# The odd layer's entry in a written-out order: x's norm first, ctx's residuals behind it, keys and values projected tile by tile with weights kept

## The chip, the cores and the metric

The kernel runs on one core of a Trainium2 chip. The metric is the device time of one execution in microseconds (us): the median of several runs. Beside it there is one profiled execution, in which the start and the length of nearly every instruction were recorded. Five engines work side by side, each through its own instructions in order: TensorE (PE, the matmuls, with the weight loads shown as PEld), VectorE (DVE), ScalarE (ACT), GpSimd (POOL) and SyncE (SP, which here only issues transfers).

## What is computed

Two transformer layers on x (512 tokens) and ctx (256 tokens), width 1024, all in float32. The layer that matters here is the second, odd one, and the end of the first one's FFN in front of it:

```python
def modulate(x, g, shift, scale):
    return rmsnorm(x, g) * (1 + scale) + shift

for l in range(2):
    ...
    a  = modulate(h,  norm1_g[l], sh1,  sc1)          # x, 512 tokens
    ac = modulate(hc, norm1_g[l], csh1, csc1)         # ctx, 256 tokens
    y, yc = even_mixer(...) if l % 2 == 0 else odd_mixer(a, ac, w_qkv, w_out, sink, cos, sin, need_ctx)
    h = h + g1 * y
    h = h + g2 * swiglu(modulate(h, norm2_g[l], sh2, sc2), ffn_w_in[l], ffn_w_out[l])
    if need_ctx:                                      # l == 0 only
        hc = hc + cg1 * yc
        hc = hc + cg2 * swiglu(modulate(hc, ...), ffn_w_in[l], ffn_w_out[l])
return rmsnorm(h, final_g)

def odd_mixer(h, hc, ...):                            # 16 query heads, 4 key/value heads, 64 wide
    q, k, v = split(h @ w_qkv)                        # rope on q and k
    kc, vc = split(hc @ w_qkv[:, 1024:])              # ctx: keys and values only, no rope
    # softmax over: keys within 128 tokens of the query (mask), all ctx keys, one sink logit per head
    ...
```

## The kernel before, in words

**Matmuls.** Every float32 product is made of three matmuls on a high and a low half in a reduced format: `mm3` (lines 106, 107, 108) multiplies high by high, high by low, low by high into one PSUM bank. An operand thus needs a high half (a cast, mostly on ScalarE) and a low half (source less high half, on VectorE or GpSimd). Activations lie transposed, eight tiles of 128 channels by 512 (x) or 256 (ctx) tokens: `hx[m]` and `hc[m]`, shown in the trace as `xT` and `ctxT`.

**Banks.** PSUM has 3 banks of tag `b` (`bank()`, shown as `pb`), 1 of tag `f` (`fill()`, `pf`), and a pool `wp` with either 2 double banks (`wide()`) or 4 single ones (`single()`), both shown as `pw`. Who asks for a bank waits until the last reader of its former content is done.

**Weights.** `unit` (line 71, called by `blocks`) loads 512 columns of a weight through SyncE into a raw buffer (`raw`, 3 of them in the odd layer's ring), casts the high half on ScalarE (line 81) and subtracts on GpSimd (line 84) into one of 4 slots (`w`). A slot comes free when its last matmul is done.

**Order.** A scheduler with a model of the engines orders most instructions within each engine. The first layer's FFN is ordered by hand instead: `run(key, fn, ...)` issues an instruction behind the last one of the same key (engine).

**The seam.** The FFN's output projection is accumulated in groups of two hidden tiles; the result of each is scaled and added to the residual by `residual` (line 774, VectorE). The units of the last hidden tile are given by a string: "e" to "j" stand for early parts of the last output group, one output tile each (`t` units, x and ctx), in which the last but one hidden tile is multiplied. Then `s2_part` does what is left of the eight x tiles and the eight ctx tiles; each is followed by `square` (line 787 on ScalarE, line 791 adds the first four to a running sum). `modulated` makes the norm, first x, then ctx: `rstd_diag` sums over channels with matmuls against ones (lines 156 and 161), forms the reciprocal root on VectorE with some small operations (lines 164, 135 and three times 137 to 139), multiplies the identity by each column of it (line 173), and `spread` (line 183) turns this with one matmul into rows over all partitions; `modulate` makes each of the eight tiles from it: `t` on VectorE (line 199), the high half on ScalarE (line 200), the low half on VectorE (line 201), shown as `ax`.

**The odd layer's entry.** For each of two key tiles `project_k` loads and splits the eight blocks of its weight, projects x and then ctx into one `wide()`, and makes rope (`rope`: shuffle, line 251, and product with cos, line 252, on VectorE; product with sin and sum, lines 253 and 254, on GpSimd) and the stacked halves (`stack_k`: `kh` on ScalarE, lines 276 and 277, `kl` on VectorE, line 279). Then the values of six token blocks are accumulated in three banks and copied out (line 1328). `project_q` (eight times) does the same as `project_k` for a query tile, with one `fill()` and `stack_q` (`qa`, `qb`, lines 261, 262 and 267). The attention follows, group by group, `softmax` (scores, line 1360 and on, mask, line 1365, maximum, line 1371, exponential, line 1374) and `attend`, with the query projections of later groups between.

Of the kernel before, what the change touches and what calls it, by code (L numbers as in the profile page):

```python
# [14 lines left out]
P = 128  # L15
# [11 lines left out]
class Builder:  # L27
# [12 lines left out]
    def load(self, pool, src, shape, name, dtype=F32, eng=None, bufs=1):  # L40
        t = pool.tile(shape, dtype, name=self.uid(name), tag=name, bufs=bufs)
        (eng or self.nc.sync).dma_start(t, src)
        return t

    def bank(self):
# [812 lines left out]
    def ffn(self, l):  # L858
# [14 lines left out]
        todo = [(1, j, k) for j in range(6) for k in range(KT)] if both else []  # L873
        tail, tiles = {}, []

        def run(key, fn, *args, **kw):

            with tc.issue_after(tail[key].ins) if key in tail else ExitStack():
                tail[key] = fn(*args, **kw)  # L879
            return tail[key]  # L880

# [165 lines left out]

        def s2_part(fs, m, W, off, n, chain=False):
            ps = self.bank()[:, :n]
# [176 lines left out]
        for u in units:  # L1226
# [10 lines left out]
            elif u[0] == "t":  # L1237
                m = u[1]
                for off, n in whos:
                    s2_part((NF - 2,), m, Wl[m][:1], off, n, True)  # L1240
            else:
                unit(*u)
            job()
        ahead = sum(u[0] == "t" for u in units)
        while jobs:
            job()
        sq = self.sumsq()
        if both:
            self.A = [self.ax() for _ in range(KT)]
        parts = ((0, TX), (TX, TC)) if both else ((TC, TC), (0, TC))  # L1250
        q0 = (4, 5)[l]
        more, sqs = [], []
        for off, n in parts:
            rest = []
            for m in range(KT):
                if m < ahead:
                    s2_part((NF - 1,), m, Wl[m][1:], off, n)
                else:
                    s2_part((NF - 2, NF - 1), m, Wl[m], off, n)
                if off == parts[0][0]:  # L1260
                    sqs.append(Tp.tile([P, 2 * NH], F32, name=self.uid("sqs"), tag="T", bufs=12))
                eng = nc.vector if both and m in (2, 3) else nc.gpsimd
                self.square(sq, m, off, n, rest, q0, sqs[m][:, off:off + n], eng)
            more.append(rest)
        if both:
            for q, (off, n) in zip(more, parts):
                self.modulated(1, sq, off, n, q)
        else:
            self.dg = Tp.tile([P, TX], F32, name="dg")
            rows = [self.final_rows(sq, q, off, n) for q, (off, n) in zip(more, parts)]  # L1270
            for r, (off, n) in zip(rows, parts):
                self.final(r, off, n)
        self.Rf.release()
        ring.release()
        Tp.release()
        if both:
            self.ada_close()

    def odd(self):
        tc, nc, a = self.tc, self.nc, self.a  # L1280
        self.wp.release()
        self.open_wide()
        self.open_ring(512, 3, 4)
        X, C = [[[t[:, c] for t in A] for A in self.A] for c in (slice(0, TX), slice(TX, TA))]
        self.hcp.release()
        Rk = tc.alloc_tile_pool(name="kv1", bufs=1, side="right", reuse_waits="tile")
        Rt = tc.alloc_tile_pool(name="rope1", bufs=1, side="right", reuse_waits="tile")
        self.ropep = Rk
        tabs = [self.load(Rk, a[n], [P, TX], n) for n in ("cos", "sin")]
        mraw = self.load(Rt, a["mask"], [P, 384], "mraw")  # L1290
        mask = Rk.tile([P, 384], F32R, name="mask")
        nc.vector.tensor_copy(mask, mraw)
        identr = Rk.tile([P, P], F32R, name="identr")
        nc.vector.tensor_copy(identr, self.ident)
        nsink = self.load(Rk, a["sink"].partition_broadcast(P), [P, 16], "sink")
        sink = Rk.tile([P, 16], F32, name="sink2")
        nc.vector.tensor_copy(sink, nsink)
        nc.vector.tensor_scalar(nsink, nsink, -1.0, None, ALU.mult)

        K = []  # L1300

        def project_k(n):
            W = self.blocks(a["k1"][n])
            kf = Rt.tile([P, TA], F32, name=self.uid("kf"), tag="kf", bufs=1)
            ps = self.wide()
            for off, T, A in ((0, TX, X), (TX, TC, C)):
                self.dense(ps[:, off:off + T], W, A)
            self.rope(ps[:, :TX], kf[:, :TX], tabs)
            nc.scalar.copy(kf[:, TX:], ps[:, TX:TA])
            K.extend(self.stack_k(kf, Rk, TA, "k1", 8))  # L1310

        for n in range(2):
            project_k(n)

        V = []
        bk = [self.bank() for _ in range(3)]
        acc = [b[:, h * TC:(h + 1) * TC] for b in bk for h in range(2)]
        for kq in range(2):
            W = self.blocks(a["v1"][kq], step=256)
            for i in range(4):  # L1320
                k = kq * 4 + i
                for tb in range(6):
                    A = [X[k][p][:, tb * P:(tb + 1) * P] if tb < 4 else C[k][p][:, (tb - 4) * P:(tb - 3) * P]
                         for p in range(2)]
                    self.mm3(acc[tb], A, W[i], k == 0 and tb % 2 == 0, k == KT - 1)
        for tb in range(6):
            v = Rk.tile([P, TC], F32, name=f"v1_{tb}")
            (nc.vector.tensor_copy if tb % 2 else nc.scalar.copy)(v, acc[tb])
            V.append(v)
        Rt.release()  # L1330
# [10 lines left out]
        def softmax(g, i, rc):  # L1341
# [9 lines left out]
            for x in range(4):  # L1351
# [10 lines left out]
                for b in range(b0, b1):  # L1362
                    if b != i:
                        m0, c = (b - i + 1) * P, st + (b - b0) * P
                        nc.tensor.matmul(ps[:, c:c + P], identr, mask[:, m0:m0 + P], start=False, stop=True,
                                         skip_group_check=True)
# [86 lines left out]
        Rs.release()  # L1453
        Rk.release()
        self.ffn_open(1)
        self.ffn_mod(1, 0)
# [98 lines left out]
```

## Time and profile before

| | |
|---|---|
| runs, us | 1605.66, 1608.77, 1609.75 (median 1608.77) |
| profiled execution, us | 1603.73, span in the profile 1601.9 |
| TensorE busy | 1524.8 us (95% of the span), weight loads 1354.8 |
| VectorE / ScalarE / GpSimd busy | 1076.4 (67%) / 722.9 (45%) / 846.9 (53%) |
| transfers | 162.00 MB, mean 101 GB/s |

The stretch that the change rewrites lies between about 916 and 1030 us from the start of the span: the last units of the FFN to 935, x's and ctx's residuals, squares and norms to 949, keys and values to 987, query projections and the first attention blocks behind that. In a line of a timeline there stand the start, the length, the engine, the line of the source, the operation, what it writes and reads, its shape and the count, and in brackets how long the engine had been idle before and what ended that. PEclk is the clock granted to TensorE as a share of full speed. A line of the waits gives who waited for whom, the total, how many times and the longest.

### The profile page before, as it was taken

The page shows a single profiled execution, that of the slowest core. Times are in us where ns is not written, and L with a number is a line of the kernel's source. Part 1 is how long each engine was busy: PE and PEld are TensorE (multiplying, and loading weights), DVE is VectorE, ACT ScalarE, POOL GpSimd, SP SyncE. Part 2 cuts the span into 40 slices and gives each one's busy share as a digit, 9 for nine tenths or more (in the row PEclk, how much of TensorE's full clock was granted, in tenths as well). Part 3 has the DMA queues.
Part 4 walks back from the last instruction along what each step waited for, and adds up shares of the span by engine and source line. Part 5 has one row for each costly group of instructions (what it writes and reads, how often), then busy time and mean ns, then how long its engine had stood idle before and what let it go on. Part 6 is the DMA issues. An engine that isn't in the chain of part 4 may idle for free.

```text
span 1601.9 us, 24950 instructions
## 1 busy us (share of the span) xinstructions
PE 1524.8 (95%) x9547; PEld 1354.8 (85%) x9547; DVE 1076.4 (67%) x1949; ACT 722.9 (45%) x1472; POOL 846.9 (53%) x574
## 2 busy tenths in 40 slices
PE   6999988999999999999999989999999899999996
PEld 4776877889988898999999978777869799999996
DVE  3720788765687888777676486665667966666656
ACT  2412676553542323332333244556655644444442
POOL 0463211061265767766776415541304688888883
PEclk9999999999999999999999999999999999999998
DMA  8845100033133334434442022110225133323301
GB/s 325 305 145 184 40 8 1 24 121 119 66 95 109 125 119 139 137 122 149 141 137 85 27 65 66 60 34 9 72 80 204 53 102 101 115 86 113 93 14 53
DMA packets 54295, 162.00 MB, mean 101 GB/s; under 512 B 6176, under 2 KB 10656, under 8 KB 46496
## 3 DMA queue, kind: packets, MB, share of 16 engines
q1 hardware_dynamic: 47120, 135.11, 25.3%
q10 hardware_dynamic: 7056, 25.30, 4.9%
q8 instruction: 75, 1.23, 0.3%
q14 instruction: 44, 0.36, 0.1%
HBM read 158.29 MB, written 2.10 MB: 100 GB/s over the span
## 4 chain that ended last, share of the span: by engine, by line
PE 79%; DVE 13%; ACT 3%; issue 3%; DMA 1%; POOL 0%; SPq 0%; POOLq 0%; DVEq 0%; ACTq 0%
PE pw L106 11%; PE pw L107 11%; PE pw L108 10%; PE pb L107 8%; PE pb L106 8%; PE pb L108 8%; PE pf L106 4%; PE pf L107 4%; PE pf L108 4%; DVE junk L228 3%; PE pb L1408 2%; PE pb L1397 2%; PE pf L359 2%; PE pw L1360 1%; DMA ar<-ada 1%
## 5 line engine op out<-in xcount | busy, mean ns | idle before, releaser
L84 POOL TENSOR_TENSOR w<-raw,w 128x512 fp32r<-128x512 f32 (+1 forms) x84 | 128.0, 1530 | 241.9 <-ACT w L81 219.2
L106 PE MATMUL pw<-ax,w 128*128 128x384 f32 (+2 forms) x732 | 233.9, 323 | 4.4 <-ACT ax L200 1.6
L107 PE MATMUL pw<-ax,w 128*128 128x384 f32 (+2 forms) x732 | 234.7, 321 | 2.0 <-DVE ax L466 1.4
L108 PE MATMUL pw<-ax,w 128*128 128x384 f32 (+2 forms) x732 | 233.7, 320 | 1.4 <-DVE w L944 1.4
L774 DVE SCALAR_TENSOR_TENSOR xT<-pb,mod,xT 128x512 f32<-128x512 f32 (+3 forms) x208 | 145.8, 706 | 118.2 <-PE pb L108 118.0
L879 POOL TENSOR_TENSOR w<-raw,w 128x512 fp32r<-128x512 f32 x114 | 179.6, 1590 | 39.6 <-ACT w L879 39.4
L879 POOL TENSOR_TENSOR w<-t,w 128x512 fp32r<-128x512 f32 x102 | 157.1, 1544 | 60.9 <-ACT w L879 60.9
L106 PE MATMUL pb<-hh,w 128*128 128x512 f32 x480 | 172.5, 359 | 7.8 <-DVE xT L774 5.2
L107 PE MATMUL pb<-hh,w 128*128 128x512 f32 x480 | 172.4, 359 | 3.5 <-POOL hh L123 2.8
L108 PE MATMUL pb<-hh,w 128*128 128x512 f32 x480 | 172.2, 359 | 0.0
L107 PE MATMUL pw<-T,w 128*128 128x384 f32 (+1 forms) x508 | 157.1, 310 | 1.2 <-DVE T L123 1.2
L108 PE MATMUL pw<-T,w 128*128 128x384 f32 (+1 forms) x508 | 157.1, 310 | 0.0
L106 PE MATMUL pw<-T,w 128*128 128x384 f32 (+1 forms) x508 | 156.4, 310 | 0.0
L106 PEld LDWEIGHTS pw<-ax,w 128*128 128x128 f32 x732 | 139.1, 191 | 12.9 <-ACT ax L200 2.4
L107 PEld LDWEIGHTS pw<-ax,w 128*128 128x128 f32 x732 | 139.4, 191 | 10.2 <-DVE ax L466 3.1
L106 PE MATMUL pf<-ax,w 128*128 128x256 f32 (+2 forms) x420 | 139.9, 333 | 8.3 <-DVE qf L252 5.5
L108 PEld LDWEIGHTS pw<-ax,w 128*128 128x128 f32 x732 | 139.4, 191 | 4.1 <-DVE w L944 1.7
L108 PE MATMUL pf<-ax,w 128*128 128x256 f32 (+2 forms) x420 | 138.8, 330 | 0.0
L107 PE MATMUL pf<-ax,w 128*128 128x256 f32 (+2 forms) x420 | 138.8, 330 | 0.0
L228 DVE SCALAR_TENSOR_TENSOR junk<-ar,cb 128x1024 bf16<-128x1024 f32 x64 | 111.1, 1735 | 8.7 <-DMA ar<-ada 8.1
L879 POOL TENSOR_TENSOR w<-rawo,w 128x512 fp32r<-128x512 f32 x60 | 108.9, 1816 | 11.9 <-ACT w L879 11.9
L879 DVE TENSOR_TENSOR hs<-hs,pw 128x384 f32<-128x384 f32 (+1 forms) x114 | 55.2, 484 | 87.3 <-PE pw L108 74.8
(377 smaller groups left out, 3938.0 us busy)
## 6 DMA issues: line engine op xcount, KB each, us to landing
raw<-ffn_in SPq DMA_DIRECT2D x44, 1024.0 KB, 5.0
ar<-ada SPq DMA_DIRECT2D x24, 1024.0 KB, 7.0
ar<-ada ACTq DMA_DIRECT2D x48, 512.0 KB, 3.5
rawo<-ffn_out SPq DMA_DIRECT2D x88, 256.0 KB, 3.0
raw<-odd_out SPq DMA_DIRECT2D x32, 256.0 KB, 2.7
raw<-qk SPq DMA_DIRECT2D x16, 256.0 KB, 7.8
raw<-uv SPq DMA_DIRECT2D x16, 256.0 KB, 2.7
raw<-even_out SPq DMA_DIRECT2D x8, 512.0 KB, 3.5
```

The lines of the kernel that those rows point to most:

```text
L84: eng.tensor_tensor(lo, raw, hi.bitcast(F32), ALU.subtract)
L106: mm(out, s[0], m[0], start=start, stop=False, **kw)
L107: mm(out, s[0], m[1], start=False, stop=False, **kw)
L108: return mm(out, s[1], m[0], start=False, stop=stop, **kw)
L228: return self.nc.vector.scalar_tensor_tensor(junk, t, 1.0, self.cb[who], ALU.mult, ALU.mult, accum_out=self.acc[who][:, col:col + 1])
L359: nc.tensor.matmul(ps[32 * q:32 * q + 32, :w], cst[:, k, :], t[:, w * q:w * q + w], start=k == 0, stop=k == KT - 1, skip_group_check=True)
L774: ins = self.nc.vector.scalar_tensor_tensor(h, ps[:, r], self.modcol(l, j, m, who), h, ALU.mult, ALU.add)
L879: tail[key] = fn(*args, **kw)
L1360: nc.tensor.matmul(ps[:, st:en], Q, K[g][p][:, b0 * P:b1 * P], start=p == 0, stop=p == 1, skip_group_check=True)
L1397: last = nc.tensor.transpose(pt[:, x * P:(x + 1) * P], es[2 * (x % 2) + x // 2][:, kb * P:(kb + 1) * P], self.ident)
L1408: nc.tensor.matmul(po[64 * h:64 * h + 64, :], V[vb][:, 64 * g:64 * g + 64], t[:, h * TC:h * TC + TC], start=kb == 0, stop=kb == nb - 1, sk ...
```

## The change

*FFN's end.* The string becomes "…s7s4efgh": four `t` units instead of six, of x alone, behind the last unit "4". What is left is done in a new `seam`: the eight x tiles with residuals and squares; ctx tiles 0 to 2 into the three banks of tag `b` (without their residuals); x's channel sums and root (`norm_root`, whose small operations have their scratch in the PSUM bank, but for the result); ctx residuals and squares 0 to 2; ctx tiles 3 to 6 into the four `single()` banks and tile 7 into a `bank()`. Everything in it is issued through `run`, thus in the order written, per engine.

*The entry.* Two rings are open at the same time, the old one (3 raw, 4 slots) for the query weights and a new one (4 raw, 8 slots) for keys and values. The eight halves of key and value weights are kept in the eight slots. The first four are loaded and split ahead of x's `norm_spread`, which makes the four products with the identity on ScalarE; the other four are loaded and split along with x's tiles. Tile by tile, x is modulated, followed by a ctx residual (tiles 0 to 4), and multiplied into both key accumulators and (tiles 0 to 3 at once, 4 to 7 later) into the values' accumulators. Behind tile 5 stands ctx's `norm_root`, behind tile 6 its `norm_spread`. Then ctx is modulated, rope follows, keys and values of ctx come last. The mask is kept as two blocks instead of three, made late with the other constants.

*Queries.* Projection 1 goes into a `bank()` instead of the one `fill()`.

```diff
@@ s2_part
-            run("DVE", self.residual, l, 5, m, off, n, ps)
+            if not late:
+                run("DVE", self.residual, l, 5, m, off, n, ps)
...
-                      ("215s6s3s7sef4ghij", "215s6s3s7sef4g")[l]):
+                      ("215s6s3s7s4efgh", "215s6s3s7sef4g")[l]):
...
-                for off, n in whos:
-                    s2_part((NF - 2,), m, Wl[m][:1], off, n, True)
+                s2_part((NF - 2,), m, Wl[m][:1], 0, TX, True)
...
+    def seam(self, s2_part, Wl, ahead):
...
+        for m in range(KT):
+            k = int(m < ahead)
+            s2_part(fs[k:], m, Wl[m][k:], 0, TX, True)
+            square(0, m)
...
+        for m in range(3):
+            c_unit(m, self.bank())
+        self.rx = self.norm_root(sq[:, :TX], self.rest1[0], TX, self.fill())
+        for m in range(3):
+            self.c_residual(m)
+        for m in range(3, 7):
+            c_unit(m, self.single())
+        c_unit(7, self.bank())
...
+    def norm_spread(self, y, T, out):
+        dg = self.tmp()
+        for j in range(T // P):
+            self.run("ACT", self.nc.scalar.mul, dg[:, j * P:(j + 1) * P], self.ident, y[:, j:j + 1])
+        self.run("PE", self.nc.tensor.matmul, out[:, :T], self.ones, dg[:, :T], start=True, stop=True)
+        return out[:, :T]
@@ odd
+        kept = self.ring, self.ring_cfg
+        self.open_ring(512, 4, 8)
...
+        W = [part(*load(v)) for v in src[:4]]
...
+        rx = self.norm_spread(self.rx, TX, self.fill())
         tabs = [self.load(Rk, a[n], [P, TX], n) for n in ("cos", "sin")]
...
+        for k in range(KT):
+            rest = mod(0, k, rx)
+            if k < 5:
+                self.c_residual(k + 3, Rt)
+            rest()
+            if k < 4:
+                W.append(part(*load(src[4 + k])))
+            k_x(k)
+            if k < 4:
+                v_x(k)
+            if k == 5:
+                rc = self.norm_root(self.sq1[:, TX:], self.rest1[1], TC, self.single())
+            if k == 6:
+                rc = self.norm_spread(rc, TC, self.single())
...
+        for k in range(KT):
+            mod(1, k, rc)()
+            if k >= 4:
+                v_x(k)
+        for n in range(2):
+            self.rope(kps[n], kfs[n][:, :TX], tabs)
+        for k in range(KT):
+            k_c(k)
...
+        for k in range(KT):
+            v_c(k)
...
         def project_q(n):
-            ps = self.fill()
+            ps = (self.bank if n == 1 else self.fill)()
```

More of the change, by code (lines that the diff above doesn't have):

```diff
@@ L1246, in ffn @@
             job()
+        if both:
+            self.seam(s2_part, Wl, ahead)
+            self.Rf.release()
+            ring.release()
+            Tp.release()
+            self.ada_close()
+            return
         sq = self.sumsq()
[L1248 to L1251, printed above, removed]
+        parts, q0 = ((TC, TC), (0, TC)), 5
         more, sqs = [], []
@@ L1261, in ffn @@
                     sqs.append(Tp.tile([P, 2 * NH], F32, name=self.uid("sqs"), tag="T", bufs=12))
-                eng = nc.vector if both and m in (2, 3) else nc.gpsimd
-                self.square(sq, m, off, n, rest, q0, sqs[m][:, off:off + n], eng)
+                self.square(sq, m, off, n, rest, q0, sqs[m][:, off:off + n], nc.gpsimd)
             more.append(rest)
[L1265 to L1272, printed above, removed]
+        self.dg = Tp.tile([P, TX], F32, name="dg")
+        rows = [self.final_rows(sq, q, off, n) for q, (off, n) in zip(more, parts)]
+        for r, (off, n) in zip(rows, parts):
+            self.final(r, off, n)
         self.Rf.release()
@@ L1298, in odd @@
[L1298 to L1310, printed above, removed]
@@ L1312, in odd @@
-        for n in range(2):
-            project_k(n)
-        V = []
[L1316 to L1325, printed above, removed]
+        with tc.issue_after(self.tail["DVE"].ins):
+            nc.vector.tensor_copy(mask, mraw.rearrange("p (a c) -> p a c", a=3)[:, 0::2, :])
+            nc.vector.tensor_copy(identr, self.ident)
+            nc.vector.tensor_copy(sink, nsink)
+            nc.vector.tensor_scalar(nsink, nsink, -1.0, None, ALU.mult)
@@ L1329, in odd @@
             V.append(v)
+        self.close_ring()
+        self.ring, self.ring_cfg = kept
+        self.wp.release()
+        self.open_wide()
         Rt.release()
@@ L1454, in odd @@
         Rk.release()
+        self.hcp.release()
         self.ffn_open(1)
```

129 lines of the change are left out of this document (110 added, 19 removed).

## The prediction

> **What bounds the kernel now.** I read the profile page first (engine shares, then the chain that ended last), next the waits of the stretch that the change rewrites, then TensorE's and the other engines' timelines there. All times are microseconds.
>
> ```profile
> PE 1524.8 (95%) x9547; PEld 1354.8 (85%) x9547; DVE 1076.4 (67%) x1949; ACT 722.9 (45%) x1472; POOL 846.9 (53%) x574
> PE 79%; DVE 13%; ACT 3%; issue 3%; DMA 1%; POOL 0%; SPq 0%; POOLq 0%; DVEq 0%; ACTq 0%
> ```
>
> TensorE is busy 95% of the span and makes 79% of the chain. The change alters hardly any matmul, so it can only move TensorE's idle time and the stretches in which its clock is low. Two of TensorE's waits between 915 and 1020 (total, times, longest):
>
> ```profile
> PE pf L106 <- DVE qf L252: 5.3, 3, 3.1
> PE pb L106 <- DVE xT L774: 0.7, 1, 0.7
> ```
>
> Three times, 5.3 in all, a query projection waits for the rope of the one before; once an FFN output part waits for a bank. TensorE's timeline places the former and adds the entry's gaps (in brackets: idle before, and what ended it):
>
> ```profile
> 939.13 1.95 PE L161 MATMUL pf<-ones,sqs 128*128 128x128 f32 x16
> 943.15 1.95 PE L161 MATMUL pb<-ones,sqs 128*128 128x128 f32 x16
> 946.51 1.10 PE L183 MATMUL pf<-q,ones 128*128 128x512 f32 x2 [1.41 <-DVE sm L164]
> 949.20 0.80 PE L106 MATMUL pw<-ax,w 128*128 128x512 f32 x1 [1.60 <-ACT ax L200]
> 951.05 0.63 PE L106 MATMUL pw<-ax,w 128*128 128x512 f32 x1
> 951.48 0.63 PE L107 MATMUL pw<-ax,w 128*128 128x512 f32 x1
> 953.08 0.51 PE L107 MATMUL pw<-ax,w 128*128 128x512 f32 x1 [0.55 <-DVE ax L201]
> 954.12 0.39 PE L106 MATMUL pw<-ax,w 128*128 128x512 f32 x1
> 954.35 0.39 PE L107 MATMUL pw<-ax,w 128*128 128x512 f32 x1
> 995.75 0.47 PE L106 MATMUL pf<-ax,w 128*128 128x512 f32 x1 [3.10 <-DVE qf L252]
> 1005.02 0.50 PE L106 MATMUL pf<-ax,w 128*128 128x512 f32 x1 [1.25 <-DVE qf L252]
> 1013.09 0.50 PE L106 MATMUL pf<-ax,w 128*128 128x512 f32 x1 [0.94 <-DVE qf L252]
> 1020.93 0.50 PE L106 MATMUL pf<-ax,w 128*128 128x512 f32 x1 [0.25 <-DVE qf L252]
> ```
>
> A 512-column matmul normally follows the last after 0.23 (954.12 to 954.35). So the entry idles for 1.41 + 1.60 + 0.55 = 3.56. After its gaps a matmul takes 0.43 (951.05 to 951.48): the clock is low. The grouped windows say so (fourth group of figures: PEclk) for the two stretches behind a long gap:
>
> ```profile
> 949.20:953.00 3.80, 3.30 (x6) 1.78 (x6) 3.80 (x7) 2.78 (x5) 2.61 (x2) 0.57 0.19 59
> 995.75:1000.20 4.45, 4.45 (x13) 3.50 (x14) 0.00 (x0) 0.00 (x0) 2.12 (x2) 0.62 0.18 59
> ```
>
> So a gap of 3.10, or 1.41 and 1.60 close together, brings about 3.4 at half clock: 8 matmuls at 0.43 for 0.23, **1.6 lost**. The gaps of 1.25 and less bring none.
>
> **The terms: the norms.** The durations:
>
> ```profile
> 942.18 0.48 DVE L774 SCALAR_TENSOR_TENSOR ctxT<-pb,mod,ctxT 128x256 f32<-128x256 f32 x1
> 942.59 0.15 DVE L139 SCALAR_TENSOR_TENSOR sm<-sm,sm 128x4 f32<-128x4 f32 x1
> 943.89 0.16 DVE L137 TENSOR_TENSOR sm<-sm 128x4 f32<-128x4 f32 x1
> 944.09 0.16 DVE L138 SCALAR_TENSOR_TENSOR sm<-sm,sm 128x4 f32<-128x4 f32 x1
> 944.48 1.88 DVE L173 TENSOR_SCALAR q<-ident,sm 128x128 f32<-128x128 f32 x4
> 947.64 1.41 DVE L199 SCALAR_TENSOR_TENSOR t<-xT,mod,pf 128x512 f32<-128x512 f32 x2 [0.23 <-PE pf L183]
> 936.19 0.40 ACT L787 ACTIVATE sq<-ctxT 128x256 f32<-128x256 f32 x1
> 936.49 0.40 ACT L787 ACTIVATE sqs<-ctxT 128x256 f32<-128x256 f32 x1
> 943.75 0.60 ACT L81 CAST w<-raw 128x512 fp32r<-128x512 f32 x1
> 949.05 1.12 ACT L81 CAST w<-raw 128x512 fp32r<-128x512 f32 x2
> 948.42 0.72 ACT L200 ACTIVATE ax<-t,mod 128x512 fp32r<-128x512 f32 x1 [4.08 <-DVE t L199]
> ```
>
> *x's norm.* Before, the sums over x end at about 941.0; the reciprocal root on VectorE, interleaved with ctx residuals, runs from 941.1 to 944.4; four ident-times-column products take 1.9; the spread starts at 946.5. In the changed order only x's early FFN parts remain, the ctx parts coming later, so x's sums end about 938.5, which is 2.5 earlier: of the 33 ctx matmuls that stood ahead of their end 18 are left (ctx units 0 to 2), 15 at 0.12 (half of 0.23, for half the columns) are 1.8, and the 0.7 of bank wait goes. After the sums stand ctx units 3 to 7, five times 6 matmuls of 0.12 = 3.6; TensorE is out of work at 942.2. Meanwhile: root, 11 operations 0.20 apart (943.89 to 944.09) = 2.2, to 941.1 with the first wait; three ctx residuals 0.41 apart = 1.2 to 942.3; the last ctx square 0.4 to 942.8. ScalarE executes in the written order: the casts of the four first key and value weights come behind those squares, 0.52 apart (1.12 less 0.60), 2.1 in all, to 944.9; then the four products, now on ScalarE. The profile of before has no such product there. Its ScalarE rows for twice that width start 0.30 apart, so I take 0.30 each, 1.2 in all (VectorE's 0.47 each would give 1.9): 946.1. So the products gain little themselves and stand behind 2.1 of casts that they do not need. The gap ahead of the spread is 946.1 − 942.2 = 3.9 (take 3.8), where it was 1.41. Spread about 0.9, first modulation 0.75 and 0.72 with handovers: the second gap is 1.8, where it was 1.60. The low half follows 0.55 later, as before, and the second accumulator waits 0.6 for a ctx residual whose bank it takes. 3.8 + 1.8 + 0.55 + 0.6 = 6.75 against 3.56: **+3.2**. One half-clock stretch in both.
>
> *ctx's norm.* Before, its sums (to 943.15 + 1.95 = 945.10) covered most of x's root, and its root ran beside the key matmuls of x: no wait of TensorE for it. In the changed order TensorE does these sums after x's tile 5: 20 matmuls at 1.95 / 16, 2.4. VectorE, in order, has the ctx root queued ahead of tile 6's modulation and stands waiting for those sums. When they end: root 2.2, modulation 0.7, ScalarE 0.72, handovers 0.5, and only then can tile 6's matmul start; nothing else is queued on TensorE between. A gap of 4.2, the low half 0.55, and, the gap being longer than 3.10, a half-clock stretch of 1.6: **+6.35**. If the clock holds: +4.75.
>
> [...]
>
> **The terms: the query stage.** Its rows:
>
> ```profile
> 988.87 5.35 DVE L279 TENSOR_TENSOR kl<-kf,kh 64x768 fp32r<-64x768 f32 x4 [0.82 <-ACT kh L276]
> 994.91 0.69 DVE L252 TENSOR_TENSOR qf<-pf,cos 128x512 f32<-128x512 f32 x1
> 1006.44 1.28 ACT L1374 ACT_TABLE_LOAD   x1 [2.68 <-DVE sa L1372]
> 1007.73 0.69 ACT L1374 ACTIVATE e<-pw,sa 128x512 f32<-128x512 f32 x1
> 1009.58 1.35 DVE L267 SCALAR_TENSOR_TENSOR qa<-qf,qa 64x512 fp32r<-64x512 f32 x1 [3.22 <-ACT qa L261]
> ```
>
> Before, query projection 1 waited 3.10: it needs the one fill bank, whose release (the rope of projection 0) stood on VectorE behind 5.35 of key low halves. Now projection 1 has a bank of its own, its weights and those of projection 0 are loaded and cast early, and the key low halves are done while values are projected. Gone: 3.10, its half-clock stretch 1.6, and the 1.25 of projection 2: −5.95. What is late next: projections 3 and 4 still share the fill bank. Projection 3 I leave at 0.9. Projection 4 waits for the rope of 3, which stands behind the softmax of the first block: table load 1.28, exponential 0.69, a cast of 0.52, the two query high halves, the low halves of 1.35 and 0.69, then shuffle and product of 0.7 each. This chain does not move with the earlier projections, so I put its wait at 2.3 where it was 0.25: +2.05. Sum **−3.9**; with a half-clock stretch behind the 2.3, −2.3.
>
> **The rest.** Early FFN parts for x alone make one residual of 512 columns follow each other more closely: 0.1, nothing. The smaller mask and the kept K and V weights save no TensorE work: the matmuls are the same, and the two input rings hold no bank of PSUM. SyncE's loads of cos and sin stand behind the second halves of the weights, which wait for free raw buffers, and are needed only by the ropes, behind all key matmuls of x. Without that cover the first rope would be late by a landing, 2.7 by the nearest row. The first attention half starts with the queues of ScalarE and VectorE fuller by the same softmax; I give it from 0 to +4, take +1.5. The landing just named, and the largest wait of TensorE between 1020 and 1150 that is there now:
>
> ```profile
> raw<-odd_out SPq DMA_DIRECT2D x32, 256.0 KB, 2.7
> PE pb L1397 <- ACT e L1374: 1.0, 3, 0.5
> ```
>
> **Sum:** 3.2 + 6.35 − 3.9 + 1.5 = 7.15, I take **+7**. The profiled execution of before took 1603.73 (span 1601.9), which is 5.0 under the median of the runs, 1608.77. So 1610.7 beside that profile, and 1615.8 as the median. The terms' ends: −1.6 without the ctx half-clock stretch, −1.5 without loss in the attention, against +1.6 and +2.5: from +3.9 to +11.1.
>
> **The rivals.** *Even out.* The gap at projection 4 and the loss in the attention do not come, and the second gap does not halve the clock: 7 − 2.05 − 1.5 − 1.6 = +1.9, or 1610.7. For it: the trace of before shows projections catching up by themselves (1.25, 0.94, 0.25). Against it: the table load and exponential are bound to the first block. Chance 0.25.
>
> *Faster.* Both norm chains stay covered: on ScalarE the products of x's norm get ahead of the ctx squares and the casts (2.1 + 1.6 less, so the first gap is near 0.1), and on VectorE tile 6's modulation gets ahead of ctx's root, so that no gap stands at tile 6. Then x's entry is worth −0.5, ctx's norm 0, and the query stage −3.9 to −5.95: −5 in the middle, or 1603.8. It decides where the time from the end of x's sums to the first key matmul is 8 or less, as in the trace of before (941.0 to 949.2), and no gap stands ahead of tile 6. Against it: the engines take their instructions in order, and the order written puts both roots and casts ahead. Chance 0.10.
>
> [...]
>
> ```profile
> 949.89 1.23 DVE L137 TENSOR_TENSOR sm<-sm 128x2 f32<-128x2 f32 x1
> 949.73 2.61 POOL L84 TENSOR_TENSOR w<-raw,w 128x512 fp32r<-128x512 f32 x2 [4.04 <-ACT w L81]
> ```
>
> A 0.16 step of the ctx root took 1.23 beside the weight subtraction. [...]
>
> *Worse.* One more half-clock stretch (behind the gap at projection 4) and +4 in the attention: 7 + 1.6 + 2.5 = +11.1, or 1619.9. Chance 0.10.
>
> *Nothing changes,* the scheduler having placed it as before: 1608.8. The instruction order does differ on every engine; 0.02.
>
> **How the numbers follow.** My forecast has 0.53. A measurement of this kernel can tell about 0.3%, 4.8, from no change: slower means above 1613.6, faster below 1603.9. Of the forecast's 0.53 some 0.05 fall under +4.8. Slower: 0.48 + 0.10 = 0.58; same: 0.25 + 0.05 + 0.02 = 0.32; faster 0.10. The range reaches from the even case less 3.7 for errors of several terms of about one each (1607) to the worse case with 1 more (1621); it leaves out the faster case and some of the worse one.
>
> **What would show it.** In the profile after: a wait of the spread matmul for the ident products on ScalarE near 3.8 between 942 and 946; the first key matmul 10 after the end of x's sums instead of 8; ctx's sums after x's tile 5 and right behind them a gap near 4.2 ahead of tile 6 with a granted clock near 0.6 after it; no wait of 3.1 at projection 1; one of about 2.3 at projection 4. I am wrong if either norm gap is under 2, or if the waits inside the first attention half grow by over 4.

## The result and the profile after

The changed kernel took 1617.53 us (median; 1616.27 to 1619.45), the kernel before 1605.99 over its six runs: 1.0071 times as long, 95% interval 1.0061 to 1.0081, so 11.5 us slower. The forecast was 1615.8, with 1607 to 1621 as range.

TensorE's waits of the changed kernel between 915 and 1030 (who waited for whom: total, times, longest). Lines have moved: L112 to L114 are the matmuls of `mm3`, L48 is whatever `run` issues.

```profile
PE pf L112 <- DVE qf L258: 5.5, 2, 4.5
PE pw L112 <- ACT ax L48: 5.3, 2, 3.7
PE pf L48 <- ACT q L48: 3.6, 1, 3.6
PE pb L112 <- DVE xT L780: 1.7, 1, 1.7
```

The prediction's 5.3 for ropes ends at 1020; in the window used here the kernel before waits

```profile
PE pf L106 <- DVE qf L252: 5.5, 4, 3.1
```

So the waits for ropes add up to 5.5 in both kernels, in two waits instead of four; the waits of the two norms are new in size. The timeline of the changed kernel on TensorE:

```profile
936.54 1.06 PE L48 MATMUL pf<-ones,sq 128*128 128x128 f32 x8
939.22 1.95 PE L48 MATMUL pf<-ones,q 128*128 128x128 f32 x16
948.39 1.37 PE L48 MATMUL pf<-q,ones 128*128 128x512 f32 x2 [3.58 <-ACT q L48]
951.36 0.79 PE L112 MATMUL pw<-ax,w 128*128 128x512 f32 x1 [1.59 <-ACT ax L48]
968.33 1.95 PE L48 MATMUL pw<-ones,csq 128*128 128x128 f32 x16
973.94 0.79 PE L112 MATMUL pw<-ax,w 128*128 128x512 f32 x1 [3.66 <-ACT ax L48]
1015.56 0.50 PE L112 MATMUL pf<-ax,w 128*128 128x512 f32 x1 [0.99 <-DVE qf L258]
1027.72 0.80 PE L112 MATMUL pf<-ax,w 128*128 128x512 f32 x1 [4.52 <-DVE qf L258]
1184.37 0.61 PE L162 MATMUL pf<-ones,sq 128*128 128x128 f32 x4
```

In order: x's sums; the gap ahead of its spread; the first key matmul; ctx's sums behind tile 5, and behind them the gap ahead of tile 6; projections 3 and 4; and the first sum of the next norm, from which on both kernels have the same instructions. The granted clock behind the three long gaps (windows; PEclk is the third figure from the end):

```profile
951.36:956.67 5.31, 5.31 (x19) 3.97 (x19) 4.52 (x8) 3.81 (x8) 3.44 (x3) 0.57 0.30 89
973.94:980.30 6.36, 6.36 (x15) 4.72 (x16) 3.50 (x6) 1.98 (x5) 0.00 (x0) 0.53 0.00 0
1027.72:1034.87 7.15, 7.15 (x24) 5.76 (x25) 3.34 (x5) 3.23 (x7) 3.14 (x3) 0.77 0.01 3
```

Three stretches at low clock in this part, where the kernel before has two; and the two in the entry are each twice as long as the one in the entry there. Here are the windows around them, the first row from the kernel before, the other two from the changed one. In the changed kernel the clock is half while it is low (0.50 from 953.0 to 955.0 and from 974.5 to 978.5), so I take the time at half clock as twice the missing share of the window: 3.4, 6.9 and 6.9 us.

```profile
949.00:952.50 3.50, 3.27 (x6) 1.78 (x6) 3.47 (x8) 2.48 (x6) 2.61 (x2) 0.51 0.07 16
949.00:956.00 7.00, 5.41 (x15) 3.30 (x14) 5.01 (x9) 3.92 (x8) 5.66 (x5) 0.51 0.44 140
973.00:980.00 7.00, 6.06 (x14) 4.46 (x15) 3.60 (x7) 2.54 (x5) 0.00 (x0) 0.51 0.00 0
```

In the trace of the kernel before the same last landmark is

```profile
1170.13 0.61 PE L156 MATMUL pf<-ones,sq 128*128 128x128 f32 x4
```

From the first sum over x to that landmark the kernel before takes 1170.13 − 935.38 = 234.75 us, the changed one 1184.37 − 936.54 = 247.83: **13.1 more in this stretch**. I call this length *the stretch* and read it the same way in every trace below: it leaves out what differs between two executions elsewhere. The spans of the two profiled executions differ by 15.8, the medians by 11.5; the changed kernel's profiled execution, 1619.45, is its longest, and that of before is shorter than any of its other runs. Of the 13.1, 7.1 is idle time of TensorE (17.3 in the stretch instead of 10.2). Another 3.6 is low clock: missing share times length of the windows shown gives 2.3, 3.0 and 1.6, against 1.6 and 1.7 in the two windows of the prediction. Six more ctx matmuls lie inside the stretch (30 instead of 24, 0.12 each), 0.7; the other 1.7 I have not traced.

One trace is one execution. The profiled executions of e2 and e6 took 3.1 and 3.4 more than their medians, and two stretches differ by 1.0 to 1.1 ahead of the place where the edit acts (e2 and e9, below). A difference of about 1 between two stretches can therefore not be read as an effect.

### The profile page after: what moved, and what is told of

Same layout as the page of the kernel before. It is cut to its first block, busy times and chain, and to the rows that moved or that the text cites. A ratio compares the mean times of both kernels' runs of the same rounds, so it can differ in the third digit from the quotient of the medians.

```text
span 1617.7 us, 24916 instructions
## 1 busy us (share of the span) xinstructions
PE 1531.5 (95%) x9547; PEld 1359.8 (84%) x9547; DVE 1071.3 (66%) x1933; ACT 725.2 (45%) x1478; POOL 847.1 (52%) x576
## 4 chain that ended last, share of the span: by engine, by line
PE 79%; DVE 12%; ACT 4%; issue 3%; DMA 1%; POOL 1%; SPq 0%; POOLq 0%; DVEq 0%; ACTq 0%
PE pw L112 11%; PE pw L113 11%; PE pw L114 11%; PE pb L113 8%; PE pb L114 8%; PE pb L112 8%; PE pf L112 4%; PE pf L113 4%; PE pf L114 4%; PE pb L1552 2%; DVE junk L234 2%; PE pb L1541 2%; PE pf L365 2%; PE pw L1504 1%; PE pw L1512 1%
## 5 line engine op out<-in xcount | busy, mean ns | idle before, releaser
L112 PE MATMUL pw<-ax,w 128*128 128x384 f32 (+2 forms) x732 | 236.4, 325 | 8.0 <-ACT ax L48 5.3
L90 POOL TENSOR_TENSOR w<-raw,w 128x512 fp32r<-128x512 f32 (+1 forms) x76 | 116.5, 1540 | 242.7 <-ACT w L87 220.6
L114 PE MATMUL pw<-ax,w 128*128 128x384 f32 (+2 forms) x732 | 234.9, 322 | 1.4 <-DVE w L945 1.4
L48 POOL TENSOR_TENSOR w<-raw,w 128x512 fp32r<-128x512 f32 x122 | 190.4, 1576 | 42.0 <-ACT w L48 41.9
L48 POOL TENSOR_TENSOR w<-t,w 128x512 fp32r<-128x512 f32 x102 | 156.2, 1535 | 62.5 <-ACT w L48 62.5
L112 PE MATMUL pb<-hh,w 128*128 128x512 f32 x480 | 172.6, 360 | 8.0 <-DVE xT L780 5.4
L114 PE MATMUL pb<-hh,w 128*128 128x512 f32 x480 | 172.6, 360 | 0.0
L114 PE MATMUL pw<-T,w 128*128 128x384 f32 (+1 forms) x508 | 157.0, 310 | 0.0
L112 PE MATMUL pw<-T,w 128*128 128x384 f32 (+1 forms) x508 | 156.3, 310 | 0.0
L112 PEld LDWEIGHTS pw<-ax,w 128*128 128x128 f32 x732 | 140.1, 192 | 17.1 <-ACT ax L48 6.5
L112 PE MATMUL pf<-ax,w 128*128 128x256 f32 (+2 forms) x412 | 137.7, 334 | 8.6 <-DVE qf L258 5.7
L114 PEld LDWEIGHTS pw<-ax,w 128*128 128x128 f32 x732 | 140.4, 192 | 4.3 <-DVE w L945 1.7
L113 PE MATMUL pf<-ax,w 128*128 128x256 f32 (+2 forms) x412 | 136.1, 330 | 0.8 <-POOL ax L129 0.8
L114 PE MATMUL pf<-ax,w 128*128 128x256 f32 (+2 forms) x412 | 135.6, 329 | 0.0
L234 DVE SCALAR_TENSOR_TENSOR junk<-ar,cb 128x1024 bf16<-128x1024 f32 x64 | 110.1, 1720 | 11.1 <-DMA ar<-ada 10.5
L48 DVE TENSOR_TENSOR hs<-hs,pw 128x384 f32<-128x384 f32 (+1 forms) x114 | 55.2, 484 | 87.9 <-PE pw L114 76.2
L48 POOL TENSOR_TENSOR w<-rawo,w 128x512 fp32r<-128x512 f32 x60 | 106.7, 1778 | 12.1 <-ACT w L48 12.1
```

Of the source, the lines that this page charges most:

```text
L48: self.tail[key] = fn(*args, **kw)
L90: eng.tensor_tensor(lo, raw, hi.bitcast(F32), ALU.subtract)
L112: mm(out, s[0], m[0], start=start, stop=False, **kw)
L113: mm(out, s[0], m[1], start=False, stop=False, **kw)
L114: return mm(out, s[1], m[0], start=False, stop=stop, **kw)
L234: return self.nc.vector.scalar_tensor_tensor(junk, t, 1.0, self.cb[who], ALU.mult, ALU.mult, accum_out=self.acc[who][:, col:col + 1])
```

## The experiments

Each time is a median; the ratio is to the kernel before on the same chip in the same runs (1605.67 for the first four, 1606.76 for the next four, 1605.87 for the last three).

| run | us | ratio, 95% interval | the stretch |
|---|---|---|---|
| before | 1605.99 | | 234.75 |
| after | 1617.53 | 1.0071 [1.0061, 1.0081] | 247.83 |
| e1, after with one bank | 1615.64 | 1.0062 [1.0049, 1.0074] | 244.86 |
| e2, before with own bank | 1606.52 | 1.0006 [0.9996, 1.0015] | 236.61 |
| e3, x's products first | 1615.26 | 1.0056 [1.0043, 1.0069] | 245.02 |
| e4, ctx's root late | 1610.03 | 1.0025 [1.0016, 1.0034] | 241.02 |
| e5, exponential's table early | 1617.21 | 1.0065 [1.0053, 1.0077] | 246.93 |
| e6, entry reordered | 1603.33 | 0.9983 [0.9974, 0.9992] | 235.25 |
| e7, e6 with one bank | 1606.13 | 0.9996 [0.9987, 1.0004] | 235.36 |
| e8, e7 with early parts split | 1606.92 | 1.0000 [0.9992, 1.0009] | 235.38 |
| e9, after, low halves split | 1617.54 | 1.0071 [1.0057, 1.0084] | 248.68 |
| e10, e6 with the table early | 1602.95 | 0.9981 [0.9973, 0.9990] | 232.57 |
| e11, e10, low halves split | 1607.28 | 1.0004 [0.9995, 1.0013] | 236.96 |

### e1 and e2: what the own bank of projection 1 is worth

e1, from the changed kernel (e2 makes the opposite edit in the kernel before):

```diff
-            ps = (self.bank if n == 1 else self.fill)()
+            ps = self.fill()
```

> The changed kernel with one line undone: query projection 1 shares the fill bank again. Theory A (the bank only moves the wait): projection 1 waits about 3.2 us again, with a half-clock stretch of 1.6 behind it, but the 4.5 us wait at projection 4 and its half-clock stretch go, since the first exponential comes no later; net within 1.5 us of the changed kernel. Rival B (the bank is worth what was predicted): 5 to 6 us slower than the changed kernel, and the wait at projection 4 stays.

> The kernel before with that line alone changed: query projection 1 gets a bank of its own. Theory A: the waits of 3.10 and 1.25 us and the half-clock stretch behind the first go (-5.95), a wait of about 4.5 us with a half-clock stretch comes at projection 4 (+5.9), and the first attention half loses some: from -1 to +3 us against the kernel before. Rival B: -3.9 to -6 us.

e1's waits for ropes between 915 and 1040, and those of e2:

```profile
PE pf L112 <- DVE qf L258: 6.2, 4, 3.1
```

```profile
PE pw L1360 <- DVE qa L267: 1.6, 1, 1.6
PE pf L106 <- DVE qf L252: 1.3, 2, 0.8
```

With one bank, e1's projection 1 waits 3.10 again, and the 4.52 at projection 4 is gone. The stretch is 3.0 shorter than in the changed kernel; by the times 1.6 less (the 0.3 between the two baselines taken off), which the intervals do not separate from nothing. In the kernel before, the own bank takes the 3.10 away and puts a wait of 1.6 for a query's low half, with a low clock behind it (0.76 from 1010.25 to 1017.42), and later ones of 0.8 and 0.5 in its place: 1.0006, no change, the stretch 1.9 longer. But 1.1 of these 1.9 stand ahead of projection 0, where the edit does nothing yet (it starts 52.7 after x's first sum instead of 51.6): the same two gaps in the entry, 1.40 and 1.60, brought 6.9 of half clock in this execution and 3.4 in that of the kernel before. That leaves 0.8 for the own bank, too little to tell. Rival B, the predicted worth of 3.9 to 6, falls in both. Against the kernel before, e1 is the entry alone: 10.1 in the stretch, 10.0 in the times.

### e3: x's products ahead of squares and casts

```diff
-        self.rx = self.norm_root(...)
+        self.rx = self.norm_diag(self.norm_root(...), TX, "t")   # the four products, at once
...
         rx = self.norm_spread(self.rx, TX, self.fill())          # this held the products; now the spread alone
```

> The changed kernel with the four products of x's norm issued on ScalarE straight behind the root, ahead of the three ctx squares and the four weight casts. Theory (they only stand in the way): the gap of 3.58 us ahead of the spread shrinks to under 0.5, 3 to 3.6 us faster than the changed kernel. Rival (the weights would be late next): the casts then end 1.3 us later and GpSimd's low halves behind them, so that the first key matmuls wait for weights and less than 1.5 us is gained.

TensorE's waits of e3:

```profile
PE pw L112 <- ACT ax L48: 6.1, 2, 3.7
PE pw L113 <- DVE ax L48: 1.1, 1, 1.1
```

The wait for the products is gone altogether (there is no line "pf <- ACT q"). But the second gap grew from 1.59 to 2.48 and the low half behind it waits 1.1: the four casts, on ScalarE since 942.62, now stand ahead of x's first tile. The two norm waits of x together fall by 1.6 (3.59 for 5.17), and the low clock behind them (0.84 from 944 to 948, 0.73 from 948 to 952) lasts 3.4 instead of 6.9. The stretch is 2.8 shorter, between theory and rival, and so are the times with 1.9. The products did stand in the way; the casts then stand in the way of the next step.

### e4: ctx's root behind tile 7

```diff
             if k == 5:
-                rc = self.norm_root(self.sq1[:, TX:], self.rest1[1], TC, self.single())
-            if k == 6:
+                cs = self.norm_sums(self.sq1[:, TX:], self.rest1[1], TC, self.single())   # matmuls alone
+            if k == 7:
+                rc = self.norm_root(None, None, TC, cs, True)                             # VectorE alone
                 rc = self.norm_spread(rc, TC, self.single())
```

> The changed kernel with ctx's root on VectorE behind tile 7's modulation and ctx's spread on TensorE behind tile 7's key matmuls; ctx's sums stay behind tile 5. Theory (the root ahead of tile 6 is the gap): no gap of 3.66 us ahead of tile 6, no half-clock stretch there, -5.3 us; ctx's tiles come later and their key matmuls wait up to 1.5 us: 3.5 to 5.5 us faster than the changed kernel. Rival (the wait moves whole to ctx's tiles): 0 to 1.5 us faster, with a gap of some 3 us ahead of ctx's key matmuls.

```profile
PE pw L112 <- ACT ax L48: 1.6, 1, 1.6
PE pf L112 <- DVE qf L258: 2.5, 2, 2.3
PE pw L1513 <- DVE qa L273: 1.2, 1, 1.2
```

The gap of 3.66 ahead of tile 6 is gone with its low clock (1.00 from 972 to 984), and ctx's 48 key matmuls take 8.06 (984.53 to 992.59) where the changed kernel needs 5.76: a wait of 2.3 for ctx's tiles. Projection 1 starts 61.9 after x's first sum instead of 66.4, 4.5 earlier, as expected. Beyond that the wait at projection 4 shrank from 4.52 to 2.26 (the scheduler put another score tile ahead of projection 3 here), which I had not expected: 6.8 in the stretch, 7.2 in the times. Of the losses taken out one at a time, this one gave back the most.

### e5: the exponential's table

```diff
+            if k == 6:
+                run("ACT", nc.scalar.activation, warm, self.ones[:, 0:1], AF.Exp)
```

> The changed kernel with one exponential of a single column on ScalarE behind tile 6's cast, so that the table load of 1.28 us is done before the attention. Theory A (the wait at projection 4 is the chain of the first softmax, the table load in it): the wait of 4.52 us shrinks by 1.3, the half-clock stretch behind it stays: 1.3 us faster than the changed kernel, 2.9 if that stretch goes too. Rival B (the chain ends on VectorE's low halves whatever the exponential does): the wait stays within 0.3 us and so does the time.

```profile
PE pf L112 <- DVE qf L258: 4.7, 2, 3.8
```

The wait fell from 4.52 to 3.75, by 0.8 of the 1.28, and its half-clock stretch stayed (matmuls 0.43 apart from 1028.61 to 1031.60, 0.23 behind that); the stretch is 0.9 shorter and the time 1.1 less beside its baseline, which the intervals do not separate from no change. Both theories are too simple: the table load is part of the chain but does not end it.

### e6 to e8: the whole entry reordered

e6 joins e3 and e4, lets the scheduler place the first four casts (it puts them ahead of x's squares) and overlaps ctx's tiles; e7 is e6 with projection 1 in the fill bank; e8 is e7 with another string for the early parts.

```diff
-        W = [part(*load(v)) for v in src[:4]]
+        W = [part(*load(v), True) for v in src[:4]]      # the cast not issued through run
...
         for k in range(KT):
-            mod(1, k, rc)()
+            rest = mod(1, k, rc)
+            if last:
+                last()                                   # low half of the tile before
+            last = rest
...
-                      ("215s6s3s7s4efgh", ...
+                      ("215s6s3s7sef4gh", ...            # e8
```

> The changed kernel with the whole entry reordered, the arithmetic as it was: the first four weight casts on ScalarE not bound to the written order (they then stand ahead of x's squares), x's products straight behind the root, ctx's root behind tile 7's modulation, and in ctx's modulation the next tile's first step ahead of the last tile's low half. Theory: the gap ahead of x's spread goes to under 0.5 us and the one behind it stays near 1.6, so -3.5; the gap at tile 6 and its half-clock stretch go, -5.3; the waits for ctx's tiles seen when only the root was moved (2.3) go too; the wait at projection 4 halves as it did there: 10 to 13 us faster than the changed kernel, 1605 to 1607 us, about the kernel before. Rival (the loss is what the own bank does to the attention, the entry's gaps only pad it): under 6 us faster.

> The reordered entry with query projection 1 in the fill bank again. Entry: -8.8 us against the run with one bank (1615.6), so 1606 to 1607; the wait of 3.1 at projection 1 with its half-clock stretch is there, waits of about 1 at projections 2 to 4, and no waits of 0.4 in the first attention half. If bank and entry add up, it is 1 to 3 us faster than the reordered entry with the own bank; if the own bank only hurts behind a late entry, it is as fast or slower.

> As the run before it, and of the four early FFN parts for x two stand ahead of the last unit again, as in the kernel before, the other two behind it. Theory (four x parts in a row wait for a bank, 1.7 us where the kernel before waits 0.7): the wait for the bank falls under 0.8, 1 us faster. Rival: the bank is late because VectorE is late, whatever the order; no change within 0.5.

All of TensorE's waits of e6 between 915 and 1040:

```profile
PE pf L112 <- DVE qf L258: 2.8, 2, 2.3
PE pb L112 <- DVE xT L780: 1.7, 1, 1.7
PE pw L112 <- ACT ax L48: 1.6, 1, 1.6
PE pw L1525 <- DVE qa L273: 1.2, 1, 1.2
PE pw L112 <- DVE ctxT L780: 0.3, 1, 0.3
PE pw L113 <- DVE ax L48: 0.3, 1, 0.3
```

The norms' gaps have gone but for the 1.6 that the kernel before has too, and in the entry the clock is at half for 3.4 (0.63 from 948 to 952, 0.94 from 952 to 956) instead of twice 6.9. The stretch is 12.6 shorter than the changed kernel's, the time 1603.33: 0.9983 [0.9974, 0.9992] of the kernel before. The order written out lost its time by where it put four groups of small instructions, and putting them elsewhere gives it back; the rival falls.

e7 brings the rope's waits back (7.5 in all, 4.5 at projection 1, since the low halves of both key tiles now stand ahead in one run of 7.7):

```profile
PE pf L112 <- DVE qf L258: 7.5, 4, 4.5
```

Its stretch is as long as e6's within 0.1, while its time is 2.8 more. So bank and entry do not add up as I had written: the own bank costs 3.0 of the stretch behind the changed entry, and nothing that can be told in the kernel before and behind the reordered entry. The two profiled executions also took the same time, 1606.70 and 1606.85; e6's is one of its longest, so its trace need not show what its median execution does, and where the 2.8 between the medians lies is open. e8 brought no gain (1606.92 against 1606.13): the wait of 1.7 became two of 0.84 and 0.85, no longer for a bank but for ScalarE's and VectorE's halves of the last hidden tile. The rival's outcome came, about as late whatever the order; its reason, a late VectorE, is shown for half of the wait at most.

### e9 to e11: which engine makes the ropes late

In the windows of the changed kernel GpSimd is full while projections run back to back (fifth busy figure, 5.00 of 5; the next 5 us, 1013 to 1018, are the same):

```profile
1008.00:1013.00 5.00, 5.00 (x24) 4.14 (x23) 4.10 (x5) 2.51 (x4) 5.00 (x5) 1.00 0.35 108
```

e9 moves one weight low half of projections 2 and 3 to VectorE; e10 is e6 with e5's edit; e11 is e10 with e9's.

```diff
+            self.dve_lo = 2 * int(n in (2, 3))
+            W = self.blocks(a["q1"][n])
+            self.dve_lo = 0
-            self.dense(ps, self.blocks(a["q1"][n]), X)
+            self.dense(ps, W, X)
```

> The changed kernel with one of the two weight low halves of query projections 2 and 3 on VectorE instead of GpSimd; the scheduler then also puts the second score tile ahead of projection 3's matmuls. Theory A (with the projections back to back GpSimd is full, 5.00 of 5 us busy in both halves of 1008 to 1018, so that the rope, and behind it VectorE's low halves and the softmax, are late): the wait of 4.52 us at projection 4 falls under 2.5 and its half-clock stretch goes, 2.5 to 4 us faster than the changed kernel. Rival B (VectorE's own queue makes it late): with more work there the wait stays above 4, no gain or up to 1 us slower.

> The reordered entry with the exponential's table loaded early. Theory A: the wait of 2.27 us at projection 4 falls to about 1, and the half-clock stretch behind it goes: 1.3 to 2.9 us faster than the reordered entry (1603.3), so 1600.5 to 1602. Rival B: as with the changed kernel, where the table cost 0.8 of its 1.28: 0.3 to 0.8 us faster.

> The run before with one of the two weight low halves of query projections 2 and 3 on VectorE as well. Theory A (GpSimd is what makes the rope late): another 1 to 2 us, 1599 to 1601. Rival B: no change within 0.5, or slower by the two instructions of 0.7 us on VectorE.

VectorE and GpSimd in e9:

```profile
1012.71 1.67 DVE L273 SCALAR_TENSOR_TENSOR qb<-qf,qb 64x512 fp32r<-64x512 f32 x1
1016.08 0.69 DVE L273 SCALAR_TENSOR_TENSOR qb<-qf,qb 64x512 fp32r<-64x512 f32 x1
1012.10 1.74 POOL L90 TENSOR_TENSOR w<-raw,w 128x512 fp32r<-128x512 f32 x1
```

In e9 the wait at projection 4 fell to 1.12, as theory A has it, but a wait of 2.16 for a query's low half and one of 1.24 at projection 3 took its place, with a low clock behind them (0.69 from 1016.11 to 1018.20, 0.66 from there to 1026.36): 1617.54, no gain (its stretch is 0.9 longer, but 1.0 of that stands ahead of projection 1, behind more low clock in the entry). The same instruction of VectorE takes 0.69 alone and 1.67 beside GpSimd's subtraction, which takes 1.74 where it takes 1.29 elsewhere. So neither theory holds as I put it: in these rows an instruction of either engine takes longer beside one of the other, and work moved from the one to the other stays in the way. e11 says the same with the good entry: 1607.28, 4.3 slower than e10.

e10 has the lowest median, 1602.95, 0.9981 [0.9973, 0.9990] of the kernel before. In its trace the wait at projection 4 is 1.05 instead of 2.27 and the low clock behind it is gone (matmuls 0.23 apart from 1011.39 on), 2.7 in the stretch as theory A expected; by the times it gains 0.4, or loses 0.5 if each is taken beside its own baseline, so the two cannot be told apart, and neither can the two theories.

## Why the prediction was right, and where not

The direction and the range were right, the size was 7 for 11.5. That 1615.8 comes as near to 1617.53 as it does is luck in part: it was reckoned from a median of 1608.77 for the kernel before, which over six runs is 1605.99. Point by point:

- *x's norm, +3.2.* The mechanism right, the parts of the size not. Forecast were gaps of 3.8 and 1.8 and the trace has 3.58 and 1.59; ScalarE's rows show the reason given, four products behind casts they do not need, and e3 confirms it:

```profile
945.00 2.16 ACT L48 CAST w<-raw 128x512 fp32r<-128x512 f32 x4
947.07 1.27 ACT L48 ACTIVATE q<-ident,sm 128x128 f32<-128x128 f32 x4
```

  But the trace lists no wait of 0.55 or 0.6 behind these gaps, so TensorE's waits grew by 1.6 and not by 3.2. And "one half-clock stretch in both" was 6.9 long where the kernel before has 3.4, which costs 0.7 more (2.3 for 1.6). That makes 2.3 for 3.2.
- *ctx's norm, +6.35.* The mechanism right, the size by luck, since two errors cancel. A gap of 3.66 (forecast 4.2) stands ahead of tile 6 right behind ctx's sums, without the 0.55 behind it; the clock is 0.53 after it and costs 3.0, not 1.6. VectorE does the root first and tile 6's first step behind it, and e4, which moves the root, removes the gap:

```profile
970.31 0.17 DVE L48 TENSOR_SCALAR pw<-pw 128x2 f32<-128x2 f32 x1 [7.04 <-PE pw L48]
972.39 0.74 DVE L48 SCALAR_TENSOR_TENSOR t<-xT,mod,pf 128x512 f32<-128x512 f32 x1
```

  The clock did not hold, nor did it behind the 3.10 of the kernel before (0.62 there): it is 1.00 from 968.0 to 973.0 and low from 973.0 on (0.51 up to 980.0), 2.7 after TensorE's last matmul at 970.3. The two norms were forecast at 9.55 together; by waits and clock they come to 9.0 (1.6 + 0.7 + 3.7 + 3.0), and e1 less the kernel before is 10.1 in the stretch.
- *The early parts, 0.* Mis-sized. The bank wait of 0.7 was to go; it is 1.71, and x's sums end at 941.2 and not at 938.5 (1.1 of that stands in this trace ahead of the change already, on matmuls that both kernels share).
- *The query stage, −3.9.* The step that failed: the stage gained nothing. Both kernels wait 5.5 for ropes between 915 and 1030, with one stretch of half clock among the projections in each. The waits at projections 1 and 2 went as forecast and projection 3 waits 0.99 for 0.9. But projection 4 waits 4.52 for 2.3, with the half-clock stretch that I had only given to the worse rival. The chain that I listed is there, but I took its lengths from a trace in which the projections were apart; back to back, GpSimd is full (5.00 of 5 from 1008 to 1013), and VectorE's low halves `qb` take up to 1.80 where the one at 1010.96 in the kernel before, with GpSimd idle, takes 0.69. The chain's two ends on VectorE in the kernel before, the maximum of the first scores and the last product of the rope behind it:

```profile
1004.88 0.68 DVE L1371 TENSOR_REDUCE sa<-pw 128x1 f32<-128x512 f32 x1
1012.34 0.69 DVE L252 TENSOR_TENSOR qf<-pf,cos 128x512 f32<-128x512 f32 x1
```

  In the changed kernel, rows of GpSimd, VectorE and ScalarE:

```profile
1015.42 0.68 DVE L1515 TENSOR_REDUCE sa<-pw 128x1 f32<-128x512 f32 x1
1016.13 0.91 DVE L273 SCALAR_TENSOR_TENSOR qa<-qf,qa 64x512 fp32r<-64x512 f32 x1
1016.45 1.75 POOL L259 TENSOR_TENSOR sh<-sh,sin 128x512 f32<-128x512 f32 x1
1017.08 1.67 DVE L273 SCALAR_TENSOR_TENSOR qb<-qf,qb 64x512 fp32r<-64x512 f32 x1
1018.78 1.14 DVE L1516 TENSOR_TENSOR sa<-sa,sink 128x1 f32<-128x1 f32 x1
1019.99 1.28 ACT L1518 ACT_TABLE_LOAD   x1 [3.42 <-DVE sa L1516]
1024.50 1.80 DVE L273 SCALAR_TENSOR_TENSOR qb<-qf,qb 64x512 fp32r<-64x512 f32 x1
1026.23 0.71 DVE L257 STREAM_SHUFFLE sh<-pf 128x512 f32<-128x512 f32 x1
1026.97 0.69 DVE L258 TENSOR_TENSOR qf<-pf,cos 128x512 f32<-128x512 f32 x1
```

  From the maximum to the end of the product the chain takes 8.15 in the kernel before and 12.24 here. Of the 4.1 more, 2.7 are two low halves of an earlier query that now stand between the maximum and the next softmax step (1018.78), the second of them 1.67 long beside GpSimd; 1.1 are the last two low halves (3.13 together instead of 2.04). The table load waits for that softmax step, and the shuffle and the product that free the bank come at 1026.23 and 1026.97, 5 and 6 after projection 3 is done. e5 and e9 show that the table load and GpSimd have a part in this wait; that either alone makes it is not shown.
- *The attention, +1.5.* In the same direction: behind 1030 the waits for exponentials are 1.6 in five instead of 1.0 in three, and two of 0.4 for GpSimd are new, 1.4 together. Query stage and attention together were forecast at −2.4; the changed kernel less e1 is +3.0 in the stretch. The listed waits explain about half of these 3.0, the rest is open.
- *The rivals.* The half-clock stretch at projection 4, of the worse rival, came true; the even one did not. The faster one's point of decision was a first key matmul 8 or less behind the end of x's sums; it is 951.36 − 941.17 = 10.2.

## What to carry to other kernels

An order written out by hand is a promise for every engine: before writing one, ask for each small step on a path (a root, a product, a cast) what stands ahead of it in its own engine's queue, and let the step that TensorE waits for go first. Here a wait that was taken away came back where the next engine was full (3.10 at projection 1 against 4.52 at projection 4, GpSimd busy 5.00 of 5), so price the gain of a freed bank by the engines behind it and not by the wait's own length; removing 3.1 us and its clock loss was worth nothing in the kernel before, and behind the slower entry the trace is 3.0 longer for it (the times, 1.6, do not settle that). And a size that comes out right can hide two errors: for ctx's norm the waits were forecast too long and the low clock too short.

## What was not expected of the hardware

The clock was granted low behind shorter single gaps than the 3.10 that I had gone by. Projection 3 of e2 stands behind a gap of 1.63, and projection 4 of e4 behind one of 2.26 (a row of the windows of each):

```profile
1010.25:1017.42 7.17, 7.17 (x26) 5.76 (x25) 4.45 (x7) 3.72 (x6) 3.30 (x3) 0.76 0.18 65
```

```profile
1020.84:1028.03 7.19, 7.19 (x24) 5.74 (x25) 2.29 (x3) 3.23 (x7) 4.79 (x4) 0.76 0.25 75
```

Both take 7.2 for 24 matmuls that take 5.44 at full clock (projection 1 of the changed kernel, 1002.94 to 1008.38). The bank wait of 1.71 in the changed kernel brought no low clock (1.00 from 925.35 to 929.35), nor did the single gap of 1.25 in the kernel before (1.00 from 1005.02 to 1010.60). Waits of 2.16 in e9 (0.69 up to 1018.20), 2.20 in e11 and 2.27 in e6 (matmuls 0.43 apart behind both, then 0.23) and the 2.26 of e4 each had low clock behind them; of 1.63 and 1.71 the one had it and the other not.

Nor does a gap cost one fixed stretch. In these traces the half clock lasts about 3.4, twice that or three times that: e2 has 6.9 behind the two gaps that brought 3.4 in the kernel before, and e9 has 10.3 behind the same x gaps, 3.58 and 1.59, that brought 6.9 in the changed kernel (0.51 over the 10.5 from 945.0 to 955.5; already the two matmuls of x's spread take 2.08 there, and 1.37 in the changed kernel). The row of e2:

```profile
953.00:960.00 7.00, 6.24 (x15) 4.36 (x15) 6.97 (x13) 3.16 (x5) 3.81 (x3) 0.51 0.42 138
```

The "1.6 lost" of the prediction is the price of the shortest; the same entry paid it once in the one execution and twice in the other, and e9's three times where the changed kernel's paid it twice, less what falls on idle time.

And instructions of VectorE and GpSimd took longer where they ran beside each other, 1.67 for 0.69 and 1.74 for 1.29 in the rows of e9, in a part where GpSimd, busy for 53% of the span before, works from 1003.8 to 1019.9 of the changed kernel without a pause.
